# Rebuilding the opening stage of a two-layer encoder kernel, and the order of weight halves in its products

## The chip, the cores and the metric

The kernel runs on one core of one Trainium2 chip. The metric is the device time of one execution in microseconds; lower is better.

## The reference

Two layers. Each derives shift, scale and gate vectors from c, mixes tokens by two attention branches and a gated merge, and then applies a squared-ReLU MLP. Cut to what matters here:

```python
c_act = jax.nn.silu(c)
for l in range(2):
    ada = c_act @ w_ada[l] + b_ada[l]                 # w_ada: 1024 x 6144
    sh1, sc1, gt1, sh2, sc2, gt2 = split(ada, 6)
    h = rms(x, g_mix[l]) * (1.0 + sc1) + sh1          # x: 256 x 1024
    parts = split(h @ w_in[l], IN_SPLITS)             # q, k, v of both branches, two gates
    y_a = gqa_attention(rope(rms(qa)), rope(rms(ka)), va) @ w_branch_a[l]
    y_b = dilated_attention(qs, ks, vs) @ w_branch_b[l]
    x = x + gt1 * ((gate_a * y_a + gate_b * y_b) @ w_out[l])
    h2 = rms(x, g_mlp[l]) * (1.0 + sc2) + sh2
    x = x + gt2 * (square(relu(h2 @ w_ff1[l])) @ w_ff2[l])
```

Everything is float32 in and out.

## The kernel before

**Products.** Tokens are two halves of 128 rows (`t`), the 1024 features eight slices of 128 (`k`). A product of float32 matrices is made of three TensorE products: every operand is split into a high part (rounded to the fp32r format) and a low part (the rest), and `mm3` (L684) adds high·high, low·high and high·low into the same PSUM bank. Weights come in tiles of 128 x 1024 (512 KB) into one of six buffers `wr`; ScalarE writes the high half of `w` (`split_next`, L659), then DVE the low half.

**The vectors from c.** `ada_tile` (L594) loads one 512 KB tile of `w_ada` into a `wr` buffer and lets DVE multiply it with `c_act`, which is c broadcast to all partitions, and sum along the row, which gives one column of shift, scale or gate. `sh_sc` (L603) adds the bias and forms (1 + scale) x g. There are 96 such tiles, spread over the whole kernel.

**The opening (L1285 to L1336).** Four small loads stand first: c, the first half of x, the constants (identity matrix, biases, gains), the second half of x; then the cosine table of `first_tables`. Three products with a tile of zeros (`WARM = 3`) run first on TensorE. c goes through silu and is broadcast by eight small products with columns of the identity. Each half of x gets its sums of squares on ScalarE (`sum_sq`), an inverse root on GpSimd, a scaling on DVE (`rms_x`), eight transposes on TensorE and two copies into `xT`. `first_tables` (L747) makes the rotary tables by products with a diagonal of gains, which ScalarE writes in eight calls of 64 columns. Then come eight steps, one for each `k`: two `w_ada` tiles (shift and scale of this slice), h and its high part on ScalarE, the low part on DVE, and two weight tiles `w_x` (chunks 0 and 1 of the q, k, v columns) and `w_y` (chunks 2 and 5). A step has 24 products of 512 columns into eight PSUM banks. After the eighth step `chunk_post` normalises and rotates the chunks, in the order 5, 2, 1, 0, on ScalarE, DVE and GpSimd, and TensorE transposes them; meanwhile TensorE has the products of chunks 3 and 4 and of the gates to do.

**The order.** No engine's order follows the text directly. Every operation is recorded, and a planner (`Plan`, L130) places them on the five engines by estimated costs, due times and free buffers (`run`, L368); for loads it models a pipe with a start time, a latency and a rate. The order that it finds is written out and fixed: each engine works its queue in that order, and a waiting instruction holds up all that stand behind it. Loads marked by `plan.first()` come first on SyncE, which issues all loads. Since the whole order is planned at once, other costs or other operations in the opening can also change the order later on.

In the profile every recorded operation has line L551, so groups are told apart by tile names: `ps` is any PSUM bank, `w` a split weight tile, `hT` the split h, `s2k` any of seven scratch tiles, `r2k` the split MLP activations.

Of the kernel before, what the change touches and what calls it, by code (L numbers as in the profile page):

```python
# [20 lines left out]
P = 128  # L21
# [11 lines left out]
AHEAD = 1  # L33
CFG = dict(ahead0=1,
  post0=(5, 2, 1, 0), s2k=7, r2k=8, ahead=1, last="k",
  dve_ss=0, hk=2,
  ada_f0=[5, 5, 0, 5, 3, 5, 0, 1, 1], ada_f1=[3, 0, 2, 0, 2, 0, 0, 1, 0],
  seq0="c3 w a v w c4 w w u w u u w a w a w w w w w w v a w w v v w w w b w y w w w b w y w y v y".split(),
  seq1="w u c2 w c3 u w c4 w u w w w a c5 w u a w w a w w v w b w v a b w w y w w v v w w w y y w w y".split())
WR = 6  # L40
NB8 = 14
WARM = 3
PSCALE = "aa"
PASSES = 4
HOLD = 400
# [84 lines left out]
class Plan:  # L130
# [237 lines left out]
    def run(self, due):  # L368
# [5 lines left out]
        wait = {e: [] for e in ORDERED}  # L374
        now = {e: [] for e in ORDERED}
        free = dict.fromkeys(ORDERED, 0.0)
        pipe = [1500.0]
        dve_port, held_port, last_plain = 0.0, (0.0, 0.0), False
        users = {name: len(u) for name, u in self.use.items()}
        began = {tag: 0 for tag in self.line}  # L380
# [32 lines left out]
        while count < n:  # L413
            moved = False
            for e in ORDERED:
# [60 lines left out]
                free[e] = t + o["occ"] + slow  # L476
                count += 1
                if e == "SP":
                    b = max(pipe[0], t + 2100.0) + o["lat"] / 380.0
                    pipe[0] = b  # L480
                    end = b + 1600.0
                else:
                    end = t + o["lat"] + slow
                heapq.heappush(ev, (free[e], 0, -1))
# [70 lines left out]
def encoder(ctx: ExitStack, tc: tile.TileContext, a: dict, out: bass.AP):  # L555
# [24 lines left out]
        return t.bitcast(F32)  # L580


    x = cp.tile([P, 2, D], F32, name="x")
    consts = cp.tile([P, P + 96 + 32 + 8], F32, name="consts")
    ident, small = consts[:, :P], consts[:, P:]
    c_act = cp.tile([P, D], F32, name="c_act")
    b_col = small[:, 0:96].rearrange("p (l w s k) -> p l w s k", l=2, w=2, s=3)
    g_col = small[:, 96:128].rearrange("p (l w k) -> p l w k", l=2, w=2)
# [43 lines left out]
    def ada_jobs():  # L632
        for l in range(DEPTH):
            for w in range(2):
                shg[l, w] = tl("sbuf", [P, 2, KT], F32, "shg", 3, f"shg{l}{w}")
                for k in range(KT):
                    for s in range(2):
                        ada_tile(l, w, s, k, shg[l, w][:, s, k : k + 1])
                        if s == 1 and (l, w) == (0, 0):
                            sh_sc(0, 0, k, k + 1)  # L640
# [44 lines left out]
        pe.matmul(ps, lh, rl, start=False, stop=stop)  # L685


    ss_of = {}

    def sum_sq(l, w, t, c):  # L690
        if c == 0:
            ss_of[l, w, t] = tl("sbuf", [P, 2], F32, "ss", 4, f"ss{l}{w}{t}")
        junk = s2k(f"junk{l}{w}{t}{c}", BF16)
        xc = x[:, t, c * 512 : (c + 1) * 512]
        o = ss_of[l, w, t][:, c : c + 1]
        if CFG["dve_ss"]:
            dve.tensor_tensor_reduce(junk, xc, xc, 1.0 / D, 0.0, ALU.mult, ALU.add, o)
        else:
            act.activation(junk, xc, AF.Square, scale=1.0 / 32.0, accum_out=o)

    def rms_x(l, w, t):
        ss = ss_of[l, w, t]
        r = ss[:, 0:1]
        with plan.keep(HOLD):
            dve.scalar_tensor_tensor(r, r, EPS, ss[:, 1:2], op0=ALU.add, op1=ALU.add)
        pool.tensor_tensor(r, r, half[:, :1], op=ALU.pow)
        for g in range(2):
            xn = s2k(f"xn{l}{w}{t}{g}")
            dve.tensor_scalar(xn, x[:, t, g * 512 : (g + 1) * 512], r, None, op0=ALU.mult)
            ps = pt(f"xT{l}{w}{t}{g}")  # L710
            for k in range(4):
                pe.transpose(ps[:, k * P : (k + 1) * P], xn[:, k * P : (k + 1) * P], ident)
            yield ps
# [34 lines left out]
    def first_tables():  # L748

        tabs = tl("sbuf", [P, 2, 2, 8, HD], F32, "b8", NB8, "tabs0")  # L750
        cs = s2k("cs").rearrange("p (o n) -> p o n", o=2)
        sp.dma_start(cs, a["cs_t"])
        gc = small[:, 128:136]
        dve.tensor_scalar(gc[:, 1::2], gc[:, 1::2], 8.0, None, op0=ALU.mult)
        e = s2k("eye")[:, :HD]
        dve.tensor_tensor(e, ident[:, 0:HD], ident[:, HD:P], op=ALU.add)
        dg = s2k("diag")
        for s in range(8):
            act.activation(dg[:, s * HD : (s + 1) * HD], e, AF.Copy, scale=gc[:, s : s + 1])
        for t in range(2):  # L760
            pss = [pt(f"tab{t}{hf}") for hf in range(2)]
            with plan.together():
                for o, (s0, s1) in enumerate(((0, 2), (2, 8))):
                    for hf in range(2):
                        rows = slice(HD * hf, HD * (hf + 1))
# [116 lines left out]
    def qkv_chunk(l, c, hT, T):  # L882
        pss = [pb(f"qkv{l}_{c}_{t}") for t in range(2)]
        for j in range(4):
            wh, wl = weights_k(2)
            for t in range(2):
                for k in range(2):
                    kk = 2 * j + k
                    lh, ll = hT.parts(kk, slice(t * P, (t + 1) * P))
                    mm3(pss[t], lh, ll, wh[:, k, :], wl[:, k, :], kk == 0, kk == KT - 1)  # L890
        for t in range(2):
            chunk_post(l, c, t, pss[t], T)

# [263 lines left out]
    def mlp(l, h2):  # L1157
# [33 lines left out]
        def ff1(j):  # L1191
# [12 lines left out]
                split_hid(r, *hid[u])  # L1204
            return hid

        def ff2_one(hid, w, j, i, t, c):
            lh, ll = (z[:, (i % 2) * S + t * P : (i % 2) * S + (t + 1) * P] for z in hid[i // 2])
            wh, wl = (z[:, c * 512 : (c + 1) * 512] for z in w)
# [72 lines left out]

    for l in range(DEPTH):
        layer_weights(l)
    c_row = cp.tile([KT, P], F32, name="c_row")  # L1285
# [14 lines left out]
    for g in range(2):  # L1300
        ps = pt(f"c{g}")
        for k in range(4):
            kk = 4 * g + k
            pe.matmul(
                ps[:, k * P : (k + 1) * P], ident[:KT, kk : kk + 1].to_broadcast([KT, P]), c_row,
                start=True, stop=True,
            )
# [89 lines left out]
def _layout(i):  # L1397
# [1 line left out]
    f = {n: np.asarray(v) for n, v in i.items()}  # L1399
    con = np.ascontiguousarray  # L1400
    r = {}
    r["x"] = con(f["x"].reshape(16, 4, 4, D).transpose(2, 1, 0, 3)).reshape(2, P, D)
    r["c"] = f["c"].reshape(KT, P)
# [11 lines left out]
    r["consts"] = con(np.concatenate([np.eye(P, dtype=np.float32), b_col, g, g0], 1))  # L1415
    cc = _chunk_cols()
    wi = f["w_in"]
    qkv = np.stack([wi[:, :, k] for k in cc], 1)
# [36 lines left out]
```

## Time and profile before

| what | value |
|---|---|
| median of 3 runs | 755.84 us (755.43 to 757.5) |
| span of the profiled execution, first to last instruction | 754.0 us |
| its time outside the span | not shown; the median lies 1.8 us above the span |
| mean granted TensorE clock | 0.995 |
| busy: TensorE, its weight loads, DVE, ScalarE, GpSimd | 739.9, 629.9, 595.4, 470.7, 70.2 us |
| transfers | 180.47 MB, mean 239 GB/s |

The span is one execution, recorded by the hardware; the runs were timed apart from it. The span is cut into stretches below to see which engine is busy in which stage; a share over the whole span says nothing about the opening, which takes the first 60 us.

### The profile page before, as it was taken

How to read it: one execution, taken by the hardware profiler on the slowest of the kernel's cores; microseconds unless marked ns; L12 is line 12 of the kernel's file. 1: busy time of each engine (PE TensorE's matmuls, PEld its weight loads, DVE VectorE, ACT ScalarE, POOL GpSimd, SP SyncE). 2: the span in 40 equal slices, each digit the busy share in tenths (PEclk: the TensorE clock that was granted, in tenths of full speed). 3: DMA queues.
4: the chain of work that ended last, by engine and by line, in shares of the span. 5: the costliest groups of instructions: out<-in, count | busy, mean ns of one | idle time of the engine just before them, and what ended most of it. 6: DMA issues, size and time to landing. Idle time of an engine off the chain costs nothing.

```text
span 754.0 us, 11447 instructions
## 1 busy us (share of the span) xinstructions
PE 739.9 (98%) x4246; PEld 629.9 (84%) x4246; DVE 595.4 (79%) x905; ACT 470.7 (62%) x784; POOL 70.2 (9%) x60
## 2 busy tenths in 40 slices
PE   7999999999999999999999999999998999999997
PEld 4888898998788888888888788889987888888886
DVE  5999999889899989566499899778879976556633
ACT  8668469785558766655256557599535865555630
POOL 0007840000000060000002111000000000000000
PEclk9999999999999999999999999999999999999999
DMA  8996379976579999666145566966635986656201
GB/s 336 385 401 208 128 246 330 356 261 234 178 283 370 386 355 341 248 223 222 58 155 182 219 242 236 363 198 212 235 140 184 344 305 224 204 191 219 88 29 56
DMA packets 50391, 180.47 MB, mean 239 GB/s; under 512 B 5624, under 2 KB 6048, under 8 KB 50336
## 3 DMA queue, kind: packets, MB, share of 16 engines
q1 hardware_dynamic: 50336, 179.75, 66.6%
q8 instruction: 33, 0.54, 0.3%
q14 instruction: 22, 0.18, 0.1%
HBM read 178.66 MB, written 1.06 MB: 238 GB/s over the span
## 4 chain that ended last, share of the span: by engine, by line
PE 84%; DVE 7%; issue 4%; ACT 3%; DMA 1%; POOL 1%; SPq 0%; POOLq 0%; ACTq 0%; DVEq 0%
PE ps L551 84%; DVE s2k L551 4%; DVE w L551 2%; ACT s2k L551 2%; DVE rstd L551 1%; DMA x<-in_x 1%; ACT pr L551 1%; ACT w L551 0%; POOL s2k L551 0%; DVE x L551 0%; DVE hT L551 0%; ACT xT L551 0%; SPq L551 0%; POOL ss L551 0%; ACT c_act L551 0%
## 5 line engine op out<-in xcount | busy, mean ns | idle before, releaser
L551 DVE TENSOR_TENSOR w<-wr,w 128x1024 fp32r<-128x1024 f32 x236 | 288.0, 1238 | 61.0 <-ACT w L551 60.6
L551 ACT ACTIVATE w<-wr 128x1024 fp32r<-128x1024 f32 x236 | 245.6, 1058 | 87.2 <-PE ps L551 48.0
L551 PE MATMUL ps<-hT,w 128*128 128x256 f32 (+1 forms) x1664 | 263.8, 315 | 0.0
L551 PEld LDWEIGHTS ps<-hT,w 128*128 128x128 f32 x1664 | 234.4, 190 | 23.6 <-issue 2.6
L551 PE MATMUL ps<-w,r2k 128*128 128x512 f32 (+1 forms) x792 | 178.8, 385 | 0.0
L551 PEld LDWEIGHTS ps<-w,r2k 128*128 128x128 f32 x792 | 144.4, 188 | 30.1
L551 PE MATMUL ps<-w,hT 128*128 128x512 f32 x672 | 163.3, 399 | 5.0 <-DVE hT L551 2.7
L551 PEld LDWEIGHTS ps<-w,hT 128*128 128x128 f32 x672 | 126.2, 191 | 33.8 <-DVE hT L551 4.5
L551 DVE CUSTOM_DVE_ANT_0 s2k<-wr,c_act 128x1024 bf16<-128x1024 f32 x96 | 117.7, 1240 | 2.3 <-DMA wr<-in_w_ada 1.6
L551 ACT ACTIVATE s2k<-ps 128x512 f32<-128x512 f32 (+3 forms) x136 | 61.5, 479 | 64.0 <-PE ps L551 55.0
L551 PE MATMUL ps<-w,mT 128*128 128x512 f32 x192 | 44.5, 391 | 0.0
L551 ACT ACTIVATE s2k<-s2k 128x512 f32<-128x512 f32 (+1 forms) x62 | 38.3, 620 | 6.0 <-DVE s2k L551 5.2
L551 PEld LDWEIGHTS ps<-w,mT 128*128 128x128 f32 x192 | 35.8, 188 | 7.3
L551 POOL TENSOR_TENSOR rstd<-rstd,half 128x8 f32<-128x8 f32 (+1 forms) x20 | 35.7, 1795 | 61.7 <-DVE rstd L551 61.7
L551 DVE TENSOR_TENSOR s2k<-ps,s2k 128x256 f32<-128x256 f32 x56 | 23.6, 421 | 17.1 <-ACT s2k L551 17.1
L551 ACT ACTIVATE pr<-pr,st 128x256 f32<-128x256 f32 (+1 forms) x64 | 35.7, 614 | 0.6 <-DVE st L551 0.6
L551 POOL TENSOR_TENSOR ss<-ss,half 128x1 f32<-128x1 f32 x8 | 4.4, 554 | 312.2 <-DVE ss L551 312.2
L551 DVE TENSOR_TENSOR r2k<-s2k,r2k 128x512 fp32r<-128x512 f32 x28 | 19.6, 699 | 15.6 <-ACT r2k L551 15.6
L551 ACT ACTIVATE s2k<-x 128x512 bf16<-128x512 f32 x16 | 10.0, 627 | 31.2 <-DVE x L551 28.3
L551 DVE TENSOR_TENSOR s2k<-ps,gtb 128x512 f32<-128x512 f32 (+1 forms) x18 | 11.8, 659 | 20.5 <-PE ps L551 18.7
L551 PE MATMUL ps<-oa,w 128*128 128x256 f32 x192 | 26.1, 288 | 0.0
L551 PE MATMUL ps<-consts,s2k 128*128 128x128 f32 x148 | 22.6, 281 | 2.9 <-DVE s2k L551 2.4
(82 smaller groups left out, 498.1 us busy)
## 6 DMA issues: line engine op xcount, KB each, us to landing
wr<-in_w_ff SPq DMA_DIRECT2D x120, 512.0 KB, 5.2
wr<-in_w_ada SPq DMA_DIRECT2D x96, 512.0 KB, 5.3
wr<-in_w_gate SPq DMA_DIRECT2D x32, 512.0 KB, 5.1
wr<-in_w_qkv SPq DMA_DIRECT2D x24, 512.0 KB, 4.6
wr<-in_w_x SPq DMA_DIRECT2D x16, 512.0 KB, 3.2
wr<-in_w_out SPq DMA_DIRECT2D x16, 512.0 KB, 5.4
wr<-in_w_y SPq DMA_DIRECT2D x8, 512.0 KB, 5.5
wr<-in_w_ba SPq DMA_DIRECT2D x8, 512.0 KB, 4.9
```

What stands on the lines that cost most here:

```text
L551: getattr(self.real[o["e"]], o["op"])(*map(real, o["a"]), **{n: real(z) for n, z in o["k"].items()})
```

## The change

- c is loaded together with its own 8 x 8 selector (`c_in`), so its broadcast no longer uses the identity matrix among the constants. The constants ride on x's rows: 144 more columns on each half of x, and their own load is gone. The load of the cosine table comes behind the first two `w_ada` tiles.
- One warm-up product in place of three.
- The second half of each row's sum of squares goes to DVE (in the first layer's opening only); the scaling of the second half of x goes to ScalarE.
- The tables' diagonal is one DVE call of 512 columns in place of eight ScalarE calls.
- Shift and scale of the first h have their own function (`first_sh_sc`) with the bias folded in; for `k = 0`, h is made by DVE in two halves, with the high part copied by ScalarE.
- `many` does high·high and low·high of several products first and high·low of all of them last. It is used in the opening's steps, in `qkv_chunk` and in the second MLP product. For `k = 0` all high·high products come first, then all low·high ones. In the last step `w_y` comes before `w_x`.
- The planner's model of loads starts at 0 in place of 1500 ns, with shorter latencies in the first 4 us and 400 in place of 380 bytes per ns.

```diff
-WARM = 3
+WARM = 1
...
-        pipe = [1500.0]
+        pipe = [0.0]
...
-                    b = max(pipe[0], t + 2100.0) + o["lat"] / 380.0
+                    quiet = t < 4000.0
+                    b = max(pipe[0], t + (1200.0 if quiet else 2100.0)) + o["lat"] / 400.0
                     pipe[0] = b
-                    end = b + 1600.0
+                    end = b + (800.0 if quiet else 1600.0)
...
-    x = cp.tile([P, 2, D], F32, name="x")
-    consts = cp.tile([P, P + 96 + 32 + 8], F32, name="consts")
-    ident, small = consts[:, :P], consts[:, P:]
+    xin = cp.tile([P, 2, D + P + 16], F32, name="xin")
+    x, ident, small = xin[:, :, :D], xin[:, 0, D : D + P], xin[:, 1, D:]
...
+    def first_sh_sc(k):
+        v, gb = shg[0, 0], b_col[:, 0, 0, 1, :]
+        if k == 0:
+            dve.scalar_tensor_tensor(gb, gb, 1.0, g_col[:, 0, 0, :], op0=ALU.add, op1=ALU.mult)
+        sc, sh = v[:, 1, k : k + 1], v[:, 0, k : k + 1]
+        dve.tensor_scalar(sc, sc, g_col[:, 0, 0, k : k + 1], gb[:, k : k + 1], op0=ALU.mult, op1=ALU.add)
+        dve.tensor_tensor(sh, sh, b_col[:, 0, 0, 0, k : k + 1], op=ALU.add)
...
+    def many(jobs):
+        for ps, lh, ll, rh, rl, start, stop in jobs:
+            pe.matmul(ps, lh, rh, start=start, stop=False)
+            pe.matmul(ps, ll, rh, start=False, stop=False)
+        for ps, lh, ll, rh, rl, start, stop in jobs:
+            pe.matmul(ps, lh, rl, start=False, stop=stop)
...
-        if CFG["dve_ss"]:
+        if on_dve:
             dve.tensor_tensor_reduce(junk, xc, xc, 1.0 / D, 0.0, ALU.mult, ALU.add, o)
...
-            dve.tensor_scalar(xn, x[:, t, g * 512 : (g + 1) * 512], r, None, op0=ALU.mult)
+            xg = x[:, t, g * 512 : (g + 1) * 512]
+            if (l, w, t) == (0, 0, 1):
+                act.activation(xn, xg, AF.Copy, scale=r)
+            else:
+                dve.tensor_scalar(xn, xg, r, None, op0=ALU.mult)
...
-        for s in range(8):
-            act.activation(dg[:, s * HD : (s + 1) * HD], e, AF.Copy, scale=gc[:, s : s + 1])
+        dve.tensor_tensor(
+            dg.rearrange("p (s n) -> p s n", s=8), e[:, None, :].to_broadcast([P, 8, HD]),
+            gc[:, :, None].to_broadcast([P, 8, HD]), op=ALU.mult,
+        )
...
             for k in range(KT):
-                push("w_x", l, k, k + 1)
-                push("w_y", l, k, k + 1)
+                for n in "xy" if k < KT - 1 else "yx":
+                    push(f"w_{n}", l, k, k + 1)
...
                     w = weights()
-                    for t in range(2):
-                        for c in range(2):
-                            ff2_one(hids[j - 1], w, j - 1, i, t, c)
+                    many([ff2_job(hids[j - 1], w, j - 1, i, t, c) for t in range(2) for c in range(2)])
...
     with plan.first():
-        sp.dma_start(c_row, a["c"])
-        sp.dma_start(x[:, 0, :], a["x"][0])
-        sp.dma_start(consts, a["consts"])
-        sp.dma_start(x[:, 1, :], a["x"][1])
+        sp.dma_start(c_in, a["c"])
+        for t in range(2):
+            sp.dma_start(xin[:, t, :], a["x"][t])
...
         for c in range(2):
-            sum_sq(0, 0, t, c)
+            sum_sq(0, 0, t, c, c == 1)
...
-    tabs_of[0] = first_tables()
+    with plan.first():
+        ada(2)
+        tabs_of[0] = first_tables()
...
-        ada(2)
+        if k:
+            ada(2)
...
-        for z in (h, hi):
-            act.activation(z, xT[:, k, :], AF.Identity, bias=v[:, 0, k : k + 1], scale=v[:, 1, k : k + 1])
-        dve.tensor_tensor(lo, h, f32(hi), op=ALU.subtract)
-        for pair in ((0, 1), (2, 5)):
+        if k == 0:
+            for t in range(2):
+                ts = slice(t * P, (t + 1) * P)
+                dve.tensor_scalar(h[:, ts], xT[:, k, ts], v[:, 1, k : k + 1], v[:, 0, k : k + 1], op0=ALU.mult, op1=ALU.add)
+                act.activation(hi[:, ts], h[:, ts], AF.Copy)
+                dve.tensor_tensor(lo[:, ts], h[:, ts], f32(hi[:, ts]), op=ALU.subtract)
+        else:
+            for z in (h, hi):
+                act.activation(z, xT[:, k, :], AF.Identity, bias=v[:, 0, k : k + 1], scale=v[:, 1, k : k + 1])
+            dve.tensor_tensor(lo, h, f32(hi), op=ALU.subtract)
+        for pair in ((0, 1), (2, 5)) if k < KT - 1 else ((2, 5), (0, 1)):
             w = weights(CFG["ahead0"])
-            for i, c in enumerate(pair):
-                wh, wl = (z[:, i * 512 : (i + 1) * 512] for z in w)
-                for t in range(2):
-                    lh, ll = hT.parts(k, slice(t * P, (t + 1) * P))
-                    mm3(pss[c][t], lh, ll, wh, wl, k == 0, k == KT - 1)
+            jobs = []
+            ...
+                many(jobs)
```

`qkv_chunk` collects its four products of a weight tile in the same way and hands them to `many`, in its last tile one half of the tokens after the other.

More of the change, by code (lines that the diff above doesn't have):

```diff
@@ L752, in first_tables @@
         sp.dma_start(cs, a["cs_t"])
-        gc = small[:, 128:136]
+        gc = xin[:, 0, D + P : D + P + 8]
         dve.tensor_scalar(gc[:, 1::2], gc[:, 1::2], 8.0, None, op0=ALU.mult)
@@ L888, in qkv_chunk @@
                     kk = 2 * j + k
-                    lh, ll = hT.parts(kk, slice(t * P, (t + 1) * P))
-                    mm3(pss[t], lh, ll, wh[:, k, :], wl[:, k, :], kk == 0, kk == KT - 1)
+                    ends = k == 1 and j == 3
+                    jobs.append((pss[t], *hT.parts(kk, slice(t * P, (t + 1) * P)), wh[:, k, :], wl[:, k, :], kk == 0, ends))
+            if j == 3:
+                many(jobs[:2])
+                many(jobs[2:])
+            else:
+                many(jobs)
         for t in range(2):
@@ L1205, in ff1, with ff2_job @@
             return hid
+        def ff2_job(hid, w, j, i, t, c):
+            lh, ll = (z[:, (i % 2) * S + t * P : (i % 2) * S + (t + 1) * P] for z in hid[i // 2])
+            wh, wl = (z[:, c * 512 : (c + 1) * 512] for z in w)
+            last = 5 if (l, t, c) == (DEPTH - 1, 1, 1) else 7
+            return accs[2 * t + c], lh, ll, wh, wl, j == 0 and i == 0, j == last and i == 3
         def ff2_one(hid, w, j, i, t, c):
@@ L1284, in encoder @@
         layer_weights(l)
-    c_row = cp.tile([KT, P], F32, name="c_row")
+    c_in = cp.tile([KT, P + KT], F32, name="c_in")
+    c_row, pick = c_in[:, :P], c_in[:, P:]
     with plan.first():
-        sp.dma_start(c_row, a["c"])
-        sp.dma_start(x[:, 0, :], a["x"][0])
-        sp.dma_start(consts, a["consts"])
-        sp.dma_start(x[:, 1, :], a["x"][1])
+        sp.dma_start(c_in, a["c"])
+        for t in range(2):
+            sp.dma_start(xin[:, t, :], a["x"][t])
     c_sig = s2k("c_sig")[:KT, :P]
@@ L1304, in encoder @@
             pe.matmul(
-                ps[:, k * P : (k + 1) * P], ident[:KT, kk : kk + 1].to_broadcast([KT, P]), c_row,
+                ps[:, k * P : (k + 1) * P], pick[:, kk : kk + 1].to_broadcast([KT, P]), c_row,
                 start=True, stop=True,
@@ L1324, in encoder @@
         hi, lo = hT.parts(k, slice(0, S))
-        for z in (h, hi):
-            act.activation(z, xT[:, k, :], AF.Identity, bias=v[:, 0, k : k + 1], scale=v[:, 1, k : k + 1])
-        dve.tensor_tensor(lo, h, f32(hi), op=ALU.subtract)
-        for pair in ((0, 1), (2, 5)):
-            w = weights(CFG["ahead0"])
-            for i, c in enumerate(pair):
-                wh, wl = (z[:, i * 512 : (i + 1) * 512] for z in w)
-                for t in range(2):
-                    lh, ll = hT.parts(k, slice(t * P, (t + 1) * P))
-                    mm3(pss[c][t], lh, ll, wh, wl, k == 0, k == KT - 1)
+        if k == 0:
[4 more added lines that the diff above has]
+                dve.tensor_tensor(lo[:, ts], h[:, ts], f32(hi[:, ts]), op=ALU.subtract)
+        else:
+            for z in (h, hi):
+                act.activation(z, xT[:, k, :], AF.Identity, bias=v[:, 0, k : k + 1], scale=v[:, 1, k : k + 1])
+            dve.tensor_tensor(lo, h, f32(hi), op=ALU.subtract)
+        for pair in ((0, 1), (2, 5)) if k < KT - 1 else ((2, 5), (0, 1)):
+            w = weights(CFG["ahead0"])
+            jobs = []
+            for t in range(2):
+                for i, c in enumerate(pair):
+                    wh, wl = (z[:, i * 512 : (i + 1) * 512] for z in w)
+                    jobs.append((pss[c][t], *hT.parts(k, slice(t * P, (t + 1) * P)), wh, wl, k == 0, k == KT - 1))
+            if k == 0:
+                for ps, lh, ll, rh, rl, _, _ in jobs:
+                    pe.matmul(ps, lh, rh, start=True, stop=False)
+                for ps, lh, ll, rh, rl, _, _ in jobs:
+                    pe.matmul(ps, ll, rh, start=False, stop=False)
+                for ps, lh, ll, rh, rl, _, _ in jobs:
+                    pe.matmul(ps, lh, rl, start=False, stop=False)
+            else:
+                many(jobs)
         if k == 3:
```

13 lines of the change are left out of this document (7 added, 6 removed).

## The prediction

> **What bounds the kernel now.** I read the page first, then TensorE's waits, then the span cut into stretches, then the chain of waits and the timeline of the opening. From the page:
>
> ```profile
> span 754.0 us, 11447 instructions
> PE 739.9 (98%) x4246; PEld 629.9 (84%) x4246; DVE 595.4 (79%) x905; ACT 470.7 (62%) x784; POOL 70.2 (9%) x60
> ```
>
> TensorE's waits over the whole span (waiter, releaser: us in total, times, longest):
>
> ```profile
> PE ps L551 <- DVE hT L551: 2.7, 4, 1.4
> PE ps L551 <- DVE s2k L551: 2.4, 7, 0.6
> PE ps L551 <- ACT hT L551: 2.3, 1, 2.3
> PE ps L551 <- DVE half L551: 1.5, 1, 1.5
> PE ps L551 <- ACT pr L551: 0.7, 1, 0.7
> ```
>
> TensorE is busy for 739.9 of 754.0 us. The change keeps all of its work but two warm-up products, so time can only move through its 14 us of idleness, through the clock, or through products that start earlier. The largest single wait is 2.3 us for the first `hT`, in the opening. The list has no row for a weight's low half (`DVE w`).
>
> The stretches (stretch, length; busy time and count of PE, PEld, DVE, ACT, POOL; granted clock, DMA share, GB/s):
>
> ```profile
> 0.00:4.50 4.50, 3.05 (x4) 1.50 (x5) 0.79 (x3) 1.59 (x2) 0.20 (x4) 1.00 0.48 165
> 4.50:7.40 2.90, 2.90 (x12) 1.44 (x12) 1.14 (x5) 2.05 (x7) 0.55 (x1) 1.00 0.88 302
> 7.40:11.90 4.50, 4.32 (x35) 3.12 (x33) 2.23 (x5) 4.49 (x14) 0.55 (x1) 1.00 1.02 418
> 12.52:15.93 3.41, 1.14 (x7) 0.58 (x4) 3.23 (x6) 3.41 (x6) 0.00 (x0) 1.00 1.02 410
> 15.93:19.34 3.41, 3.41 (x10) 2.48 (x9) 3.41 (x7) 3.41 (x6) 0.00 (x0) 0.50 1.02 402
> 19.34:60.40 41.06, 41.06 (x183) 33.89 (x181) 38.52 (x66) 25.82 (x36) 0.49 (x1) 1.00 1.02 391
> 60.40:81.00 20.60, 20.15 (x116) 16.93 (x115) 20.30 (x34) 17.04 (x31) 19.06 (x18) 1.00 0.57 187
> 572.30:575.71 3.41, 1.74 (x10) 0.94 (x8) 2.81 (x6) 2.64 (x7) 0.00 (x0) 1.00 0.69 247
> 575.71:579.12 3.41, 3.41 (x10) 2.83 (x11) 3.34 (x7) 1.84 (x4) 0.00 (x0) 0.50 0.04 17
> ```
>
> From 19.34 to 60.40 TensorE never stops: 41.06 / 183 = 0.224 us for a product of 512 columns. But DVE is busy in 38.52 of those 41.06 us and the DMA engines are full at 391 GB/s: three resources are nearly even in the eight steps of the opening, and an earlier start is worth only what all three can follow. Twice a stretch of 3.41 us in which TensorE was little busy (1.14 and 1.74 us) is followed by one with a granted clock of 0.50; with products in it, that costs 3.41 / 2 = 1.7 us.
>
> The chain of waits up to the first weight product (start, length, what), some short pieces left out:
>
> ```profile
> 2.06 5.32 DMA x<-in_x
> ...
> 7.41 2.53 ACT s2k L551 x9
> 9.93 0.96 ACT c_act L551 x2
> 10.89 0.97 ACT xT L551 x2
> ...
> 12.84 0.91 ACT w L551
> 13.75 0.85 issue
> 14.60 0.62 ACT hT L551
> ...
> 15.27 1.11 PE ps L551 x3
> ```
>
> From 7.41 on ScalarE is the bound: sums of squares, the diagonal, `c_act`, copies and weight halves stand in its one queue, and the first product starts at 15.27.
>
> **The change, part by part.** Rows for its terms, from the timeline (start, length, engine, what):
>
> ```profile
> 1.45 4.93 PE L551 MATMUL ps<-warm 128*128 128x512 f32 x6 [1.45 <-DVE half L551]
> ...
> 5.77 0.81 ACT L551 ACTIVATE s2k<-s2k,consts 128x64 f32<-128x64 f32 x3
> ...
> 6.31 2.05 PE L551 MATMUL ps<-c_row,consts 8*128 8x128 f32 x16
> ...
> 6.73 0.88 DVE L551 TENSOR_SCALAR s2k<-x,ss 128x512 f32<-128x512 f32 x2 [0.67 <-POOL ss L551]
> ...
> 8.65 1.29 ACT L551 ACTIVATE s2k<-s2k,consts 128x64 f32<-128x64 f32 x5
> ...
> 9.01 0.55 POOL L551 TENSOR_TENSOR ss<-ss,half 128x1 f32<-128x1 f32 x1 [2.32 <-DVE ss L551]
> ...
> 11.86 1.14 PE L551 MATMUL ps<-s2k,s2k 64*128 64x128 f32 x8
> ...
> 12.08 1.22 DVE L551 CUSTOM_DVE_ANT_0 s2k<-wr,c_act 128x1024 bf16<-128x1024 f32 x1
> ...
> 12.70 2.02 ACT L551 ACTIVATE w<-wr 128x1024 fp32r<-128x1024 f32 x2
> ```
>
> *ScalarE's queue.* The diagonal's eight calls go (0.81 + 1.29 = 2.1 us), and two of the four sums of squares go to DVE. `c_act` needs only c: one warm product takes 4.93 / 3 = 1.6 us, to 3.1, and sixteen passes 2.05 us, or 4.1 at half clock, so the two copies are done by 8.3 instead of 10.89. In exchange ScalarE scales the second half of x.
>
> *Bytes.* The constants now ride on x's rows, one transfer fewer on SP's queue; the cosine table moves behind the first two `w_ada` tiles. The first `w_x` tile stays the last of the same 3.02 MB (c, x 1.05, constants 0.14, table 0.26, two `w_ada` 1.05, `w_x` 0.52). By 7.40 there were 4.50 x 165 + 2.90 x 302 = 1.62 MB, the other 1.40 MB at 418 GB/s end at 10.75. In the old order ScalarE took the tile up at 12.70 without waiting. So it lands between 10.75 and 12.70, and no earlier than before; I take the middle, 11.7. High half 2.02 / 2 = 1.0, then 0.4 for two short copies of h: first product at 13.1 (12.2 to 14.1).
>
> *DVE's queue, and the added wait.* DVE now takes a sum of squares of each half of x. The second one waits for x's second half (7.38, the end of the DMA piece in the chain), and behind it stand the scaling of the first half, the diagonal's one call, and both `w_ada` sums; TensorE's transposes wait for that. From 7.4: sum 0.6 (half of a 1024-column 1.22), scaling 0.9, diagonal and root sums 0.8 by the same widths, two `w_ada` 2.4, small calls and h 0.8: 12.9, then the high part. That meets the weight tile: both paths give 13.1 to 13.2. Behind it come h's low parts and step 1's sums, no later than in the old order, since all that stands before them ends sooner.
>
> *TensorE before the first product.* x's second half: 7.4, ScalarE's sum 0.8, POOL 0.8 with its gaps (0.55 busy), scaling by ScalarE 1.2, transposes and the last table (1.14): 12.3, and 1.1 more at half clock. It fits, barely. Start: **2.1 us earlier** (15.27 to 13.2; 1.2 to 3.1).
>
> *Clock.* Before, one stretch at 0.50 lay on products and took 1.7 us. Now TensorE does little between 6 and 9, so the half-clock stretch should come earlier, over transposes and tables, where it delays the first product by up to 1.1. I take 0.5 saved; the bounds are 1.7 saved and 1.7 lost (two such stretches). The Trainium skill, "TensorE: Matmul & The Clock Gate", Part 1, says the throttled clock is the default, released only after about 3.4 us of sustained activity, in windows that run free of the kernel. This speaks against cutting the warm-ups; the two rows at 0.50 agree with the window's length. By it alone the first 3.4 us of products would run at half clock here too, nothing would be saved, and the sum would be 0.5 less.
>
> *Last step and what follows.* In the last step chunks 2 and 5 now come first, so their sums are ready 12 x 0.224 = 2.7 us before the end. The new order puts the transposes of chunk 2's second half 12 + 20 products and four transposes behind these sums (7.7 us); before, 43 products behind. Rows of that place:
>
> ```profile
> 59.91 1.43 POOL L551 TENSOR_TENSOR s2k<-s2k,tabs 128x256 f32<-128x256 f32 x2 [50.34 <-ACT s2k L551]
> 61.30 1.65 POOL L551 TENSOR_TENSOR rstd<-rstd,half 128x8 f32<-128x8 f32 x1
> ...
> 65.69 5.35 POOL L551 TENSOR_TENSOR rstd<-rstd,half 128x8 f32<-128x8 f32 x3
> ...
> 71.50 0.63 PE L551 MATMUL ps<-consts,s2k 128*128 128x128 f32 x4 [0.25 <-ACT w L551]
> ...
> 96.31 0.33 PE L551 MATMUL ps<-consts,pr 128*128 128x128 f32 x1 [0.74 <-ACT pr L551]
> ```
>
> They need two copies (1.0), two rotations (1.43 each), two powers (1.65 to 5.35 / 2 = 2.7 each) and under 1 us on DVE: 7.9 to 10. TensorE is in order, so it stands 0.2 to 2.3 us there, middle 1.2; the old order's waits of 0.25 and 0.74 may go. Net **0.2 lost** (1.0 saved to 2.3 lost).
>
> *High halves first* (`many`): it could only remove waits for low halves, of which there is none, and it adds no instruction: 0. If h's low part were late it could cost its wait, which the old order bore as well. The changed costs of the planner only move the order: the order of TensorE differs up to about matmul 910 and from 2455 to 2880 of some 4070, the last 1190 are the same. I put 0 there, bounded by half of the 2.4 us of `DVE s2k` waits either way.
>
> Sum: -2.1 - 0.5 + 0.2 = -2.4; profiled span 754.0 to 751.6. The median of the runs, 755.84, lies 1.8 above this span (the profiled execution's time outside the span isn't shown); I keep the 1.8: **753.4**, own range 752.0 to 754.6.
>
> **The rivals.**
> 1. *Supply becomes the bound.* A step's four tiles (2.10 MB) take 5.36 us at 391 GB/s, its 24 products 5.39, and DVE is 94% busy. For: these are even, and the last tile isn't loaded sooner. Against: TensorE never waited. If supply runs 4% slower than products, 8 x 0.2 = 1.7 us come back: 755.1.
> 2. *The place behind chunk 2* costs its full 2.3 us and nothing vanishes later: 753.4 + 2.1 = 755.5. For: POOL is busy 19.06 of 20.60 us there. Against: it starts some 5 us earlier.
> 3. *The start doesn't move*, since `w_x` lands no earlier and the half clock holds up the tables: 755.8.
> 4. *More than forecast*: no half clock on products (1.7), POOL's head start removes the later waits (1.0): 2.1 + 1.7 + 1.0 = 4.8, 751.0.
> 5. *Slower*: the idle place behind chunk 2 throttles the clock. It decides when TensorE is busy for 1.74 us or less of a 3.41 us window, as at 572.30. Start gains only 1.2; two half-clock stretches in the opening instead of one, +1.7; 2.3 of waiting; a throttled stretch after it, +1.7: +4.5, 760.3; with one of these terms absent 758 to 759.
>
> **How the numbers follow.** A measurement of this kernel can tell 0.3%, 2.3 us, from no change: under 753.6 is faster, over 758.1 slower. Forecast 0.46 (0.30 of it under 753.6, as it lies so near), rival 4 0.20: faster 0.50. The rest of the forecast 0.16, rival 1 0.14, rival 2 0.10, rival 3 0.03: same 0.43. Rival 5: 0.07. The range 750.6 to 756.6 takes in rivals 1 to 4 and leaves out rival 5 and the ends of rival 4.
>
> **What would show it.** First weight product near 13.2, DVE's first `w_ada` sum near 9.7, the step after the opening (about 58 instead of 60.40), one 0.50 stretch mostly before the products, no more than 2 us of waiting before 81. The forecast is wrong if the first product comes after 14.1, if ScalarE or TensorE wait for `wr` tiles in the last steps, or if waits behind chunk 2 exceed 2.3 us.

## The result, and the profile after

The changed kernel is slower: 763.59 us median against 756.67 us in the same session (ratio of the runs 1.0087, 95% interval 1.0065 to 1.0109). Forecast were 753.4 us and a range of 750.6 to 756.6. One of its four executions took 2574 us: it is left out of the ratio, and without it the median is 763.16.

From the page of the changed kernel, and then its list of TensorE's waits (waiter, releaser: us in total, times, longest):

```profile
span 761.3 us, 11423 instructions
...
PE 744.5 (98%) x4242; PEld 632.5 (83%) x4242; DVE 595.9 (78%) x912; ACT 469.4 (62%) x774; POOL 68.1 (9%) x60
```

```profile
PE ps L552 <- DVE s2k L552: 3.8, 10, 0.6
PE ps L552 <- DVE hT L552: 3.5, 5, 1.5
PE ps L552 <- DVE warm L552: 1.5, 1, 1.5
PE ps L552 <- ACT s2k L552: 1.3, 1, 1.3
PE ps L552 <- DVE rstd L552: 1.2, 1, 1.2
```

The span grew by 7.3 us. TensorE has four records fewer (two warm-up products of two records) and is yet busy 4.6 us longer (744.5 - 739.9), which points to the clock; the other 2.7 us are idleness. Two waits are new, of 1.3 and 1.2 us. The stretches (stretch, length; busy time and count of PE, PEld, DVE, ACT, POOL; granted clock, DMA share, GB/s) and TensorE's timeline around the opening's end show where:

```profile
15.29:59.30 44.01, 43.80 (x192) 35.33 (x191) 40.90 (x69) 27.51 (x38) 0.20 (x1) 1.00 0.99 378
59.30:68.57 9.27, 7.02 (x33) 5.01 (x31) 8.57 (x17) 9.27 (x20) 9.24 (x10) 1.00 0.21 69
68.57:75.40 6.83, 5.99 (x15) 4.77 (x16) 6.41 (x11) 2.87 (x6) 6.75 (x7) 0.50 0.63 218
```

```profile
63.59 0.66 PE L552 MATMUL ps<-xin,s2k 128*128 128x128 f32 x4
64.00 1.40 PE L552 MATMUL ps<-w,hT 128*128 128x512 f32 x5
66.74 0.39 PE L552 MATMUL ps<-hT,w 128*128 128x256 f32 x1 [1.34 <-ACT s2k L552]
67.53 0.63 PE L552 MATMUL ps<-xin,s2k 128*128 128x128 f32 x4 [0.41 <-DVE s2k L552]
69.41 0.45 PE L552 MATMUL ps<-xin,s2k 128*128 128x128 f32 x1 [1.25 <-DVE rstd L552]
```

Behind the opening ScalarE is busy all of 9.27 us and GpSimd 9.24, with the sums of the opening's chunks. TensorE stands three times: for a PSUM bank that ScalarE still reads (1.34), for chunk 2's second transposes (0.41) and for chunk 1's first (1.25). Then follow two stretches of 3.41 us at half clock. Before, this place had one wait of 0.25 us and full clock.

The opening itself, on TensorE:

```profile
1.48 2.08 PE L552 MATMUL ps<-warm 128*128 128x512 f32 x2 [1.48 <-DVE warm L552]
3.49 3.78 PE L552 MATMUL ps<-c_in 8*128 8x128 f32 x16
...
9.16 2.27 PE L552 MATMUL ps<-xin,s2k 128*128 128x128 f32 x8 [0.41 <-DVE s2k L552]
11.36 2.08 PE L552 MATMUL ps<-s2k,s2k 64*128 64x128 f32 x8
13.37 0.92 PE L552 MATMUL ps<-xin,s2k 128*128 128x128 f32 x4
14.22 1.14 PE L552 MATMUL ps<-s2k,s2k 64*128 64x128 f32 x8
15.29 3.94 PE L552 MATMUL ps<-w,hT 128*128 128x512 f32 x16
```

The first weight product starts at 15.29, as before (15.27). The passes for c take 3.78 us in place of 2.05, and the first tables 2.08 where the second ones take 1.14: the granted clock is half up to 13.96. (The trace has no clock record before that, 5.69 in the kernel before, and a stretch without one prints as 1.00.) Yet the opening ends 0.8 us earlier than before.

Starts on TensorE, in us rounded up to 0.01, from the timelines of the profiled executions (the first product of chunk 3 marks the opening's end; the last four columns are experiments told below):

| stage begins | before | after | a_due_old | a_due | b_new | b_r400 |
|---|---|---|---|---|---|---|
| first weight product | 15.27 | 15.29 | 15.33 | 15.92 | 16.54 | 16.34 |
| first product of chunk 3 | 60.73 | 59.94 | 60.05 | 61.32 | 62.10 | 61.92 |
| first `w_branch_a` product (`oa,w`) | 144.02 | 148.81 | 141.85 | 144.09 | 147.66 | 145.10 |
| second MLP product, layer 1 of 2 | 225.34 | 231.32 | 223.90 | 228.23 | 229.50 | 227.72 |
| `oa,w`, layer 2 of 2 | 509.23 | 516.65 | 507.69 | 514.04 | 515.33 | 513.16 |
| last product | 749.92 | 757.38 | 748.44 | 753.17 | 754.96 | 754.43 |

So 5.6 of the 7.5 us are lost between the opening's end and `oa,w` (the two stretches at half clock make 6.83 / 2 = 3.4 of them, the waits most of the rest), and 2.6 in small pieces from there to 510 us, where all that the change did to the operations is `many`.

### The profile page after: what moved, and what is told of

Same layout as the page of the kernel before. It is cut to its first block, busy times and chain, and to the rows that moved or that the text cites. A ratio compares the mean times of both kernels' runs of the same rounds, so it can differ in the third digit from the quotient of the medians.

```text
span 761.3 us, 11423 instructions
## 1 busy us (share of the span) xinstructions
PE 744.5 (98%) x4242; PEld 632.5 (83%) x4242; DVE 595.9 (78%) x912; ACT 469.4 (62%) x774; POOL 68.1 (9%) x60
## 4 chain that ended last, share of the span: by engine, by line
PE 71%; DVE 12%; ACT 6%; DMA 5%; issue 4%; POOL 0%; POOLq 0%; ACTq 0%; DVEq 0%; SPq 0%
PE ps L552 71%; DVE s2k L552 6%; DVE w L552 4%; DMA wr<-in_w_ada 3%; ACT s2k L552 2%; ACT pr L552 2%; ACT w L552 1%; DMA wr<-in_w_gate 1%; DMA wr<-in_w_y 1%; DMA wr<-in_w_qkv 1%; DVE rstd L552 1%; DVE hT L552 0%; DVE st L552 0%; ACT hT L552 0%; POOL ss L552 0%
## 5 line engine op out<-in xcount | busy, mean ns | idle before, releaser
L552 PE MATMUL ps<-w,hT 128*128 128x512 f32 x672 | 165.4, 401 | 3.5 <-DVE hT L552 3.5
L552 POOL TENSOR_TENSOR rstd<-rstd,half 128x8 f32<-128x8 f32 (+1 forms) x20 | 33.3, 1669 | 63.6 <-DVE rstd L552 63.5
L552 PE MATMUL ps<-xin,s2k 128*128 128x128 f32 x148 | 24.5, 297 | 5.9 <-DVE s2k L552 3.8
L552 PEld LDWEIGHTS ps<-xin,s2k 128*128 128x128 f32 x148 | 18.0, 150 | 13.1 <-DVE s2k L552 5.6
L552 ACT ACTIVATE s2k<-xin 128x512 bf16<-128x512 f32 x14 | 8.8, 629 | 32.1 <-DVE xin L552 29.5
```

Source lines behind the costliest of these rows:

```text
L552: getattr(self.real[o["e"]], o["op"])(*map(real, o["a"]), **{n: real(z) for n, z in o["k"].items()})
```

## The experiments

Names that begin with a_ start from the changed kernel, those with b_ from the kernel before. A ratio is to the kernel before, with its 95% interval.

### The opening's clock and the idle place

**a_warm3**

```diff
     for _ in range(WARM):
         pe.matmul(cold, warm[:, :P], warm, start=True, stop=True)
+    for _ in range(2):
+        pe.matmul(cold, warm[:, :P], warm, start=True, stop=True)
+        plan.ops[-1]["occ"] = plan.ops[-1]["lat"] = 1.0
```

> The changed kernel with three warm-up products in place of one; the order of every engine is otherwise that of the changed kernel. Theory A (the single warm-up leaves TensorE at half clock up to 13.96 us, which takes the gain of the rebuilt opening): the granted clock is 1.0 from about 5 us on, the tables and transposes take half as long, the first weight product starts near 14.0 in place of 15.29, and the time falls by 1 to 1.5 us. Theory B (the loss is made behind the opening, by waits at 63 to 69 us and the two half-clock stretches that follow): the start may move, but the waits behind chunk 2 stay at 3 us or more and at least one half-clock stretch follows them; the time falls by no more than 1.5 us of the 7. Rival C (the clock of the opening is indifferent since loads and DVE set the first product): 15.3 and no change.

Measured: 762.21 us, 1.0093 (1.0073 to 1.0112). Theory A fell in this form. The clock was full at 6.52, but c's passes moved from 3.49 to 6.74, and the clock was at half again from 9.93 to 16.76; the first product came at 17.38. The opening ended only 1.1 us later (61.06) than with the first product at 15.29. Behind it the three waits stayed (1.34, 0.40 and 1.27 us), with a half-clock stretch, as theory B had it.

**b_warm1**: `WARM = 3` to `WARM = 1` in the kernel before.

> The kernel before with one warm-up product in place of three; every order is otherwise that of the kernel before. Theory A: the clock stays at half through the c products, transposes and tables, up to about 14 us; the c products take 4.1 in place of 2.05 us and the first weight product starts 1 to 2 us later than 15.27, but the half-clock stretch at 15.93 to 19.34 goes (-1.7 us): together 0.7 us faster to 0.3 us slower. If this were the source of the loss of 7 us it would have to be slower by several us. Rival C: no change at all, first product at 15.3.

Measured: 756.63 us, 1.0003 (0.9994 to 1.0012). First product 1.45 us later and no half-clock stretch behind it, as theory A had it; in the profiled execution the opening ended 0.9 us later (61.63), which the median does not show. The warm-ups are worth nothing measurable here, either way.

**a_fill**

```diff
+        for name, n in [("g0_0", 6), ("qT0_2_1", 1), ("qT0_1_0", 5)]:
+            at = (TensorE's first operation that writes this tile)
+            into = (the open sum of chunk 3)
+            for _ in range(n):
+                add(at, "PE", "matmul", into, zero_r[:, :P], zero_r, start=False, stop=False)
```

> The changed kernel with twelve products of zeros (224 ns each, added to the open sums of chunk 3, so that they change nothing) put into TensorE's queue where it stood idle: six ahead of the gate product at 66.74 us, one ahead of chunk 2's second transposes, five ahead of chunk 1's first. All other work and orders are those of the changed kernel. Theory B1 (the idle place lets the clock gate close: 7.0 us busy of 10.1, then 6.83 us at half clock): the clock stays at 1.0 from 68 to 76 us, the 3.4 us come back, and the time is 3 to 3.5 us less; the waits' own 3 us stay. Rival B2 (the half clock there has another cause, such as the transfers or the chip's state): half clock in the same place, no change or up to 0.5 us more.

Measured: 759.81 us, 1.0059 (1.0045 to 1.0072). That is 2.1 us under the changed kernel by the ratios (1.0087 to 1.0059, with intervals that touch) and 3.9 by the profiled spans (761.3 to 757.4); 2.9 of the 3.9 are there at `oa,w` (145.94), and the rest includes a half-clock stretch at 584 us that this run does not fill. The same place in its stretches:

```profile
59.30:68.57 9.27, 9.11 (x45) 7.19 (x43) 8.35 (x18) 9.27 (x20) 9.26 (x10) 1.00 0.18 62
68.57:75.40 6.83, 6.72 (x30) 5.08 (x29) 6.62 (x11) 2.60 (x5) 6.75 (x7) 1.00 0.63 206
```

Products that compute nothing keep the clock at 1.00, and 30 products and transposes are done where 15 were. So the idleness is what closes the clock gate (the throttle that halves the granted clock): B1 holds in its mechanism, though the time fell by less than its 3 to 3.5 us. By the ratios a third of the loss was clock. (The making of the zero tile put the first product 1.0 us later, at 16.28; the opening ended at 59.95 all the same.)

**a_noswap**: the last step in the old order, `w_x` before `w_y`, chunks 0 and 1 first.

> The changed kernel with the last step of the opening in the old order: w_x before w_y, chunks 0 and 1 before 2 and 5. The whole order is planned anew. Theory B (chunk 2's sums come first, so that its slow rotation and transposes stand in TensorE's queue too early): the waits at 63 to 69 us shrink to under 1.5 us, no half-clock stretch follows, and the time falls by 4 to 6 us, to the kernel before's level or 1 us under it. Theory D (high halves first, or the planner's constants, make the loss): it stays within 1.5 us of the changed kernel. The opening itself should be the same: first product 15.3, half clock up to 14.

Measured: 759.58 us, 1.0048 (1.0030 to 1.0066). The waits for chunk 2 go, but the new plan has another: 2.89 us at the opening's end, for a bank that ScalarE frees only after other copies, and a half-clock stretch behind it. A better order by 3 us, not the kernel before's level.

**b_fill**: eight zero products ahead of the first weight product and six ahead of the product that waits at 573.5, in the kernel before.

> The kernel before with zero products (128x512) in two idle places of TensorE: eight ahead of the first weight product, while it waits for h at 13 to 15.3 us, and six ahead of the product that waits at 573.5 to 575 us. All else as before. Theory B1 (an idle place of some 2 us closes the clock gate for the next 3.41 us): the half-clock stretches at 15.93 and 575.7 go, 1.7 us each, and the time falls by 2.5 to 3.4 us to about 753. Rival B2 (the gate closes for another cause): no change, or 0.3 us slower through the added products.

Measured: 755.22 us, 0.9988 (0.9978 to 0.9998). Both half-clock stretches went, but only 0.9 us of the 2.5 to 3.4 came. Two stretches of the opening, first in the kernel before, then in this one:

```profile
15.30:20.00 4.70, 4.70 (x14) 3.56 (x15) 4.70 (x8) 4.24 (x7) 0.00 (x0) 0.64 1.03 406
...
25.00:30.00 5.00, 5.00 (x24) 4.14 (x23) 4.91 (x11) 2.68 (x4) 0.00 (x0) 1.00 0.98 389
```

```profile
15.30:20.00 4.70, 4.21 (x18) 3.04 (x18) 4.67 (x10) 4.03 (x7) 0.00 (x0) 1.00 1.05 375
...
25.00:30.00 5.00, 4.59 (x20) 3.16 (x19) 4.82 (x8) 3.28 (x5) 0.00 (x0) 1.00 0.95 358
```

At full clock TensorE does 18 products where it did 14, and then waits (4.59 of 5.00 us busy) for what loads and DVE have not yet made: the 97th product starts at 38.83, before at 38.80. Up to there the half clock lay under the supply and cost nothing. Later the filled opening was the slower one: between 30 and 50 us it moved 359 and 364 GB/s (before 383 and 394) and ended at 62.00, 1.3 us later; from 510 us to the last product 1.6 us came back. Why the loads were slower is not shown, and so the 0.9 us can't be split between the two places.

### The order

**a_due** and **a_due_old** give the planner the kernel before's plan for TensorE alone; the other engines follow by due time. The planner makes one pass in place of four, which no run tests apart.

```diff
-        best = start = None
-        for _ in range(PASSES):
+        best = None
+        for i in seq:
+            start[i] = (start of the same operation in the kernel before's plan)
+        for _ in range(1):
```

> The changed kernel in all its parts, but the planner places TensorE's operations by the times at which the kernel before's plan starts them, in place of times of its own. Theory B (the loss of 7 us is made by the order that the planner finds for the changed kernel from the end of the opening on: waits of 3 us at 63 to 69, half clock after them, longer interleaving of transposes and products, small waits up to 560 us): the cluster at 63 to 69 goes, the waits behind 80 us and the attention transposes are back at the kernel before's level, and the time lies within 2 us of the kernel before's 756.05. Rival D (the loss is made by the rebuilt opening's own operations or by high halves first): it stays 4 us or more above. Rival E (the start gives nothing, so the best that this order can do is the kernel before): not under 755.

> As the run above, and the planner's model of loads back at the old constants (start at 1500 ns, 2100 + 1600 ns, 380 bytes per ns). Theory F (the new constants let the planner expect the end of the opening at 56.6 us, 3 us before it came at 59.9, so that orders behind it are laid for the wrong moment): waits right behind the opening are smaller than with the new constants, and the time is 0.5 to 2 us under the run above. Rival (the constants only shift all times alike): within 0.5 us of the run above.

Measured: a_due 758.88 us, 1.0031 (1.0014 to 1.0047); a_due_old 754.24 us, 0.9975 (0.9961 to 0.9989). The whole change with the old order and the old constants is faster than the kernel before by 1.9 us. Theory B's cluster went in both, but a_due stayed 2.7 us above the kernel before where B had said 2 at most; the constants cost 4.6 us, more than F had said. TensorE's waits, first of a_due, then of a_due_old:

```profile
PE ps L560 <- DVE s2k L560: 2.6, 7, 0.6
PE ps L560 <- ACT pr L560: 2.3, 3, 1.5
...
PE ps L560 <- ACT v L560: 0.7, 1, 0.7
PE ps L560 <- ACT hT L560: 0.5, 1, 0.5
```

```profile
PE ps L560 <- DVE s2k L560: 2.2, 6, 0.6
...
PE ps L560 <- ACT v L560: 0.7, 1, 0.7
```

With the new constants TensorE waits for ScalarE's probabilities (`pr`, one of them 1.52 us at 491) and for h; the profiled execution also had a half-clock stretch behind a wait at 208 us.

**a_old**: the changed kernel with the old constants and an order of its own. **b_new**: the kernel before with the new constants.

> The changed kernel with the planner's old constants for loads, and TensorE's due times its own again. So far: own due times and new constants 763.6, the kernel before's due times and new constants 758.9, the kernel before's due times and old constants 754.2. Theory F1 (the new constants alone make the bad order): back near 755. Theory F2 (the planner finds a bad place for chunk 2's transposes in either model as soon as the opening is rebuilt, and only the kernel before's order of TensorE avoids it): waits of 2 to 5 us at 63 to 90 us and probably a half-clock stretch, 757 to 762.

> The kernel before with the planner's new constants for loads and nothing else of the change. Theory F1: 2 us or more slower than the kernel before, by waits behind the opening and up to 560 us. Theory F2: the same within 1.5 us, since the constants alone do not make the bad place; small waits at 470 to 560 us may come.

Measured: a_old 760.54 us, 1.0077 (1.0059 to 1.0096), with a wait of 2.04 at 65 and one of 0.86 at 70 us and a half-clock stretch; b_new 759.77 us, 1.0062 (1.0043 to 1.0080), with one wait of 1.86 at 75 us and a half-clock stretch. F1 fell for a_old, F2 for b_new: either half of the change, the operations or the constants, is enough to lose the good order.

**b_r400** changes one number in the kernel before, `o["lat"] / 380.0` to `o["lat"] / 400.0`. **b_due_new** has the three new constants and the old due times of TensorE.

> The kernel before with one number of the planner changed: 400 in place of 380 bytes per ns for a load. No operation changes, only the order that is found. Theory H (the kernel before's order is one of the better ones, and a newly planned order is worse by chance, whatever made the planner look anew): 1 to 5 us slower, by waits in places of their own. Rival (the start constants of the planner, not the rate, made b_new's 4.7 us): within 0.5 us of the kernel before.

> The kernel before with the planner's three new constants, TensorE's operations placed by the kernel before's own start times. Theory I1 (the new constants hurt through the orders of DVE, ScalarE and the loads, laid for loads that come too early): 2 to 5 us slower than the kernel before, as with the changed kernel (758.9 against 754.2). Theory I2 (they hurt through TensorE's order alone): within 1 us of the kernel before.

Measured: b_r400 761.24 us, 1.0078 (1.0060 to 1.0095); b_due_new 761.25 us, 1.0070 (1.0052 to 1.0088). Theory H holds, and so does I1, both with a loss somewhat over the 5 us that they allowed. In b_r400 every operation is the kernel before's, and 5.9 us are gone. Its page against that of the kernel before (PE 739.9):

```profile
span 758.5 us, 11436 instructions
...
PE 744.3 (98%) x4246; PEld 630.5 (83%) x4246; DVE 595.1 (78%) x905; ACT 471.5 (62%) x784; POOL 62.3 (8%) x60
```

No wait of it is over 1.5 us. By the table 1.2 us are lost by the opening's end, where the clock was at half from 10.26 to 17.08 and the first product came 1.1 us later; nothing more up to `oa,w`; and 3.4 in small pieces from there to the end, which I haven't traced one by one. In b_r400, in b_new, in b_due_new (62.88) and in a_due against a_due_old the opening ends 1.2 to 2.2 us later than without the new constants; in the changed kernel against a_old it is 0.2. b_due_new waits 2.3 us for `pr` at 493 us and 1.6 for one `s2k`, though TensorE keeps the old due times: there the constants act through the orders of ScalarE, DVE and the loads.

### High halves first, and the opening alone

**b_many** puts `many` into the kernel before; **a_nomany** makes `many` do `mm3`'s order in the changed one; **a_open** is a_due_old with neither `many` nor the swap of `w_y` and `w_x`. The first step (`k = 0`) keeps its own new order in the last two.

> The kernel before with high halves first (many) in the opening, in the q, k, v chunks and in the second MLP product, and nothing else of the change. Rival D (high halves first make the loss, for example because the sums of the opening's last step all end together): 3 to 7 us slower than the kernel before. Theory B: a product costs the same (0.229 us in the second MLP product in both), so what can differ is the new plan's waits: within 1.5 us of the kernel before.

> The changed kernel with every product's three passes together again (mm3's order), all else as changed, planned anew. Theory D (high halves first make part of the loss): 757 or less. Theory H: one more newly planned order, 757 to 764, with waits behind chunk 2 again.

> The rebuilt opening alone: one warm-up product, c with its selector, constants on x's rows, sums and scaling moved, the diagonal in one call, but no high halves first, the last step in the old order, the planner's old constants, and the kernel before's due times for TensorE. If the opening itself makes the gain of 1.9 us of the run with everything else (754.2), it is within 0.8 us of that; if high halves first share in it, 755 to 756.

Measured: b_many 755.19 us, 0.9987 (0.9973 to 1.0000); a_nomany 763.37 us, 1.0110 (1.0081 to 1.0139); a_open 755.16 us, 0.9995 (0.9986 to 1.0005). High halves first make none of the loss. The opening alone gains nothing that is measured; what a_due_old has over it (0.9975) is shared with `many` and the swap, and the two intervals overlap at their ends. In its profiled execution a_open was 2.4 us ahead of the kernel before at `oa,w` (141.61), as a_due_old was (141.85), and lost 1.7 of it to a half-clock stretch at 207 us. b_many was planned anew too and lost nothing: of seven newly laid orders (the changed kernel's, a_noswap, a_old, a_nomany, b_new, b_r400, b_many) it is the one that isn't worse.

### A version that beats both

**a_best**: a_due_old with zero products ahead of the first transposes, of the first tables, and at 573 us. **a_best2**: a_due_old with five at 206 and six at 573 us.

> The version at 754.2 (changed kernel, the kernel before's due times for TensorE, old constants) with zero products of 128x512 in three idle places of TensorE: one ahead of the first transposes at 7.3 us, two ahead of the first tables at 9.6 to 10.2, six ahead of the product that waits at 573 us. Theory A2 (the clock gate is what holds the first weight product at 15.3: 5.1 us of tables and transposes stand ahead of it, 4.2 of them at half clock): the clock is full from about 11 us, the first product starts near 13.7, and if loads can follow, the opening ends 1.5 us earlier; with the stretch at 574 gone (1.7 us) the time is near 751.5. Rival G (loads set the opening's end): the first product comes earlier, but the opening's end stays within 0.5 us of 60.0, and the time is near 752.8.

> The version at 754.2 with zero products in the two idle places that h of the MLP makes: five at 206 us in the first layer, six at 573 us in the second; none in the opening. Theory B1 (each of these places closes the clock gate in some executions, by the phase of the 3.41 us windows, for 1.7 us each): no half-clock stretch between 16 and 750 us, the median 752 to 753, the runs closer together than the 4 us of the version without. Rival B2 (the zero products delay what they cover by as much as they save): 754.2 again.

Measured: a_best 753.72 us, 0.9976 (0.9967 to 0.9985); a_best2 753.62 us, 0.9974 (0.9961 to 0.9986). In a_best the first product starts at 14.78, the opening's end stays at 60.06 (60.05): rival G holds for the opening, though not with its 752.8. The stretch at 574 went, one at 207.5 came. In a_best2 there is none between 13.8 and 751 us, and its ten runs lie within 2.4 us (a_due_old's eleven within 3.9), but the ratio is a_due_old's: the median did not follow, for which no run shows the cause. All three are about a quarter of a per cent faster than the kernel before.

## Why the prediction was wrong

- **"The changed costs of the planner only move the order ... I put 0 there, bounded by half of the 2.4 us."** This is the step that failed: a newly laid order was priced at nothing. b_r400 and b_new changed nothing but these costs and lost 5.9 and 4.6 us; a_due against a_due_old puts them at 4.6 in the changed kernel. Nor is it the costs as such: a_old has the old ones back and still loses 5.4 us, and a_due_old, with the old due times for TensorE as well, loses nothing. What the new order cost in the changed kernel is waits and half clock behind the opening, 5.6 of the 7.5 us before `oa,w`. The bound was taken from waits in the old order, but a new order makes waits that the old one doesn't have. The difference of TensorE's order up to matmul 910 was in front of me and was priced as a detail.
- **The last step and the place behind chunk 2, 0.2 net, at most 2.3.** Mis-sized: 1.34 + 0.41 + 1.25 = 3.0 us of waits. The path was followed for chunk 2's rotations alone; the bank that ScalarE still read and chunk 1's transposes weren't in it. And the clock came on top: a_fill puts what they set off at 2.1 us by the ratios and 2.9 in the trace. Rival 5 named this mechanism, with a throttled stretch behind it, but as one stretch, not two, with a chance of 0.07, and its 760.3 is still 3.3 us short.
- **First product 2.1 us earlier.** It came at 15.29. "It fits, barely", with 1.1 us more at half clock, was the weak point: at half clock were c's passes, twelve transposes and the first tables, some 9 us of TensorE's queue. The Trainium skill, "TensorE: Matmul & The Clock Gate", Part 1, has the throttled clock as the default, which the prediction set against cutting the warm-ups. The trace agrees in this (half clock up to 13.96 with one warm-up product, up to 5.69 with three), but the first weight products ran at full clock. The prediction had counted one half-clock stretch in the opening before, as the stretches print it; those of the first 5.69 us were not in its count.
- **What the start is worth.** The sum took it whole. First products at 14.23 (a_open), 14.78 (a_best), 15.33 (a_due_old) and 16.28 (a_fill) all gave an opening's end of 59.7 to 60.1. From 16.28 the 192 products ran without a wait, in 43.7 us, so an earlier start had to wait: for supply, and in the first three for ScalarE's `v` (0.7 us at the end). Rival 1's mechanism, supply, holds here: what the rebuilt opening gains, 0.7 to 1.0 us at the opening's end, comes behind the first product, not through it.
- **Clock, 0.5 saved.** About right in the changed kernel: the stretch on the products is gone, the first 24 take 5.6 us in place of 7.2, and 0.8 of these 1.6 us are left at the opening's end. That it helps only as far as supply follows is what b_fill shows: there the stretch went too, and the 97th product moved by 0.03 us.
- **`many` at 0.** Right: b_many, a_nomany.

## What to carry to other kernels

Where a planner or scheduler lays the whole order, a change of its costs is a change of every engine's queue, and its price has to be read stage by stage from the new order, not bounded by the waits of the old one; keep the old order as a control, so that the operations and the order can be told apart. A gain at the first product counts only as far as loads and the vector engine can follow. An idle place of 1.3 us or more on TensorE should be priced with the half clock that can follow it.

## What was not expected of the hardware

- Small products do not hold the clock: sixteen passes of 8 rows kept TensorE busy from 3.49 to 7.27, all through one window (3.72 to 7.14, in steps of 3.41 back from 13.96), and the next was still at half, and in a_warm3 a window with 2.05 us of them and 0.8 us of other work (6.52 to 9.93) was followed by half clock, as was in b_r400 one that was busy throughout, with 2.0 us of them (6.84 to 10.26).
- Gaps far shorter than a window close the gate. The Trainium skill, "TensorE: Matmul & The Clock Gate", Part 1, has the clock fall back after an idle window of about 3.4 us. Here waits of 1.34, 0.41 and 1.25 us with work between them, and single ones of 1.33 to 1.5 us, were followed by half clock; the measurement decides.
- Whether an idle place costs a stretch depends on where the windows of 3.41 us fall: the wait of 1.33 us in front of the MLP was followed by half clock in a_due (at 210 us) and not in a_due_old, though the two waits are equal; the one at 573 us was in a_due_old and not in a_due. The Trainium skill, "TensorE: Matmul & The Clock Gate", Part 1, says that the windows run free of the kernel, which agrees. Laid in steps of 3.41 us from a change of the clock, the windows of the 18 traces bound it, behind the opening and as an estimate for this kernel: in the 20 that half clock followed, TensorE was busy for 0.52 to 1.86 us; of those that kept full clock the least busy had 1.84, 1.85 and 1.93. The way back takes more: 2.57 us of work at half clock (68.57 to 71.98, changed kernel) were followed by a second half-clock stretch.
